# Decoder step: one PSUM bank per head in the weights-times-values, and grouped small products in both attentions

## The chip, the cores and the metric

The kernel runs on one core of a Trainium2 chip. The metric is device time in microseconds (us) of one execution; the time before is the median of three runs, 1080.63 us (1078.81 to 1083.95). Lower is better.

## The reference, cut to what matters

Two trunk layers of a decoder, for a prompt of 256 positions and 8 samples of 8 positions (320 columns in all, model width 1024), in fp32. Each layer is a mixer, then a cross-attention into 256 memory tokens with 4 heads of 256, then a squared-ReLU MLP. The mixer of layer 0 is gating plus retention; that of layer 1 is a sliding-window attention with 16 query heads and 4 key/value heads of 64.

```python
def cross_attend(h, mk, mv, w_mq, w_mo):
    q = (h @ w_mq).reshape(b, l, MEM_HEADS, MEM_HEAD_DIM)
    s = einsum('blhd,bmhd->bhlm', q, mk) * (MEM_HEAD_DIM ** -0.5)
    p = softmax(s)
    o = einsum('bhlm,bmhd->blhd', p, mv)
    return o.reshape(b, l, MEM_HEADS * MEM_HEAD_DIM) @ w_mo

def sink_attention(q, k, v, valid, sinks):
    s = einsum('...qkgd,...skd->...kgqs', q, k) * (C_HEAD_DIM ** -0.5)
    s = where(valid, s, -inf)
    p = softmax(concat([s, sink]))[..., :-1]
    return einsum('...kgqs,...skd->...qkgd', p, v)
```

The prompt attends to memory keys and values that the kernel computes itself (`mem_kv`); the samples attend to cached ones. In layer 1 the prompt attends to itself in blocks of 128, the samples to cached rows of 128 positions (`wk`, `wv`). A last RMSNorm gives `y`.

## The kernel before, in words

**Products.** X lies with features on partitions and the 320 columns in the free dimension. All large products are made in three passes with values split into a high and a low part: each weight block of 1 MB comes by one DMA from `ws` into one of three `stage` buffers (or, for the keys of the table `EXTRA`, into a free buffer of the tiles HH or HL), ACT rounds it to `whi`, DVE subtracts to `wlo` (two instructions of each per block, lines 143 to 147), and TensorE runs high by high, high by low and low by high. `gemm2` (line 188) takes such a block through 48 matmuls: 16 steps j of three. `gemm_tok` (line 214) does the same with the weights as the moving operand, 512 wide; a block is 24 matmuls there, in four steps of six, and j counts those as 0, 4, 8, 12.

**Order.** `hook(i, f, j=...)` (line 178) puts small work f behind step j of the i-th block from now; so the small products of the attentions stand between the matmuls of some large product that doesn't need them. The program order gives a priority; which instruction stands where in an engine's queue is fixed by the tile framework when the kernel is built, by its own estimate of when each is ready and when a buffer is free. Every engine runs its queue in order. Banks of PSUM come from two sets of four, `mm` for the large products and `at` for all others. `in_order` keeps the order as written. The plan (`_plan`, line 1390) lists the blocks in the order in which they are used; `weights` (line 157) stages and splits one block ahead, and stages up to two cached blocks that stand behind it.

**Cross-attention** (`cross`, line 586). For the samples, `kc` (line 469) multiplies cached keys with a block-diagonal tile Z: 16 matmuls for a block of 1 MB, four at a time in four 32-column strips of the array, all blocks of a pair of heads hp into one bank; `sample_softmax`, `sample_tr` (two transposes), then `vc` (line 541) the same way with cached values, whose fourth block scales the sum into the tile `ot`. For the prompt, `s1` makes scores and softmax, `s2` transposes the weights into PT (high part) and PL (low part), and `pv(hp)` (line 556) multiplies with the values: first two transposes of `ot` into a bank tp, then for each head of the pair and each half dc of its width a bank of its own, six matmuls 256 wide, an ACT copy to OH and a DVE subtraction to OL; last the copy and subtraction from tp into the columns 256 to 319 of OH and OL. `mo` (line 581) is the output product; its first matmul reads all 320 columns of OH of the first head, so it needs the copy from tp too. In layer 0 (`ahead` False) `kc(0,0)` and `kc(0,1)` are hooked into the last query product, `kc(0,2)` and `kc(0,3)` into the second key product, `vc(0,0)` and `vc(0,1)` into the last value block; the rest of the values work follows the value products. In layer 1 all of it stands behind the query products.

**Sliding attention** (lines 1111 to 1325). `w1(n, gp)` makes the scores of a block of 128 queries into four `at` banks and the softmax (DVE: add mask and take the maximum, later scale; ACT: exponentials) into one tile; `w2f(n, gp, kv)` turns one key/value head's weights by four transposes into a bank and copies it with ACT to a tile `pt` (tag `w2`, five buffers); `w3(n, gp, pr)` multiplies the turned weights of two heads with the values, two 64-column strips at a time, and copies to OH and OL. `ws_scores`, `ws_tr` and `ws_pv` do the same for the samples. Before, `w2f` comes in pairs and `w3` one by one, hooked into `qk_group` (N = 320), `mk` (N = 256) and `mv` (512 wide).

**End.** Three 128-row pieces of y (the last of 64 rows) are scaled in halves by DVE and ACT, and each half goes out by its own DMA of SP (lines 1385 and 1386).

Of the kernel before, what the change touches and what calls it, by code (L numbers as in the profile page):

```python
# [9 lines left out]
F32 = mybir.dt.float32  # L10
F32R = mybir.dt.float32r
I32 = mybir.dt.int32
AF = mybir.ActivationFunctionType
ALU = mybir.AluOpType
# [3 lines left out]
P = 128  # L18
NT = 320
NPR = 256  # L20
# [53 lines left out]
def decoder_step(ctx: ExitStack, tc: tile.TileContext, d, plan):  # L74
    nc = tc.nc
    V, A, G, T, S = nc.vector, nc.scalar, nc.gpsimd, nc.tensor, nc.sync
# [7 lines left out]
    def sb(shape, tag, bufs=1, dt=F32):  # L84
        cnt[0] += 1
        return pool.tile(list(shape), dt, tag=tag, bufs=bufs, name=f"{tag}_{cnt[0]}")

    def bank(kind="mm"):
        cnt[0] += 1
        return pmm.tile([P, 512], F32, tag=kind, bufs=4, name=f"{kind}_{cnt[0]}")  # L90
# [10 lines left out]
    def cvc(name, i=0, n=1):  # L101
# [6 lines left out]

    WEIGHTS = ("w_in", "w_out_e", "w_qkv", "w_out_o", "w_mq", "w_mk", "w_mv", "w_mo", "w_up", "w_down")
    EXTRA = {("vc", 0, 0, 0): "HH", ("vc", 0, 0, 1): "HL", ("vc", 0, 1, 0): "HH", ("vc", 0, 1, 1): "HL",  # L110
             ("vc", 1, 0, 0): "HH", ("vc", 1, 0, 1): "HL", ("vc", 1, 0, 2): "HH", ("vc", 1, 0, 3): "HL", ("mem",): "k8a"}
    at = [0]
    staged, halves = {}, {}
# [64 lines left out]
    def hook(i, *fs, j=7):  # L178
        while len(late) <= i:
            late.append([])  # L180
        late[i].extend((j, f) for f in fs)
# [259 lines left out]
    class Cross:  # L441
# [114 lines left out]
        def pv(self, hp):  # L556
            if hp == 0:
                self.OH = sb([P, KC, NT], "HH", 2, F32R)
                self.OL = sb([P, KC, NT], "HL", 2, F32R)
            tp = bank("at")  # L560
            for dc in range(2):
                T.transpose(tp[:, dc * P:(dc + 1) * P], self.ot[:, hp, dc * P:(dc + 1) * P], ident)
            for h2 in range(2):
                h = 2 * hp + h2
                for dc in range(2):
                    c = 2 * h + dc
                    po = bank("at")
                    for mc in range(2):
                        vh, vl = [t[:, mc, c * P:(c + 1) * P] for t in (self.VH, self.VL)]
                        T.matmul(po[:, :NPR], vh, self.PT[:, h, mc], start=(mc == 0), stop=False)  # L570
                        T.matmul(po[:, :NPR], vh, self.PL[h][:, mc], start=False, stop=False)
                        T.matmul(po[:, :NPR], vl, self.PT[:, h, mc], start=False, stop=(mc == 1))
                    A.activation(self.OH[:, c, :NPR], po[:, :NPR], AF.Copy)
                    V.tensor_tensor(self.OL[:, c, :NPR], po[:, :NPR], self.OH[:, c, :NPR].bitcast(F32), op=ALU.subtract)
            c = slice(4 * hp, 4 * hp + 4)
            oh, ol = [t[:, c, NPR:NT].rearrange("p (h d) t -> p h d t", h=2) for t in (self.OH, self.OL)]
            tv = tp[:, :256].rearrange("p (d h t) -> p h d t", d=2, h=2)
            A.activation(oh, tv, AF.Copy)
            V.tensor_tensor(ol, tv, oh.bitcast(F32), op=ALU.subtract)
# [6 lines left out]
    def cross(l, nm, mem, nn, ahead):  # L586
        c = Cross(l, nm, mem, nn)
        c.start()
        if not ahead:
            hook(2, lambda: in_order(mem.prep, (1,)))  # L590
            hook(3, lambda: in_order(mem.prep, (2,)))
        hook(3, lambda: c.kc(0, 0), lambda: c.kc(0, 1))
        if ahead:
            hook(0, lambda: ahead_of(("vc", 1, 0, 2), ("vc", 1, 0, 3)))
        for g in range(4):
            c.mq(g)
        if ahead:
            c.kc(0, 2)
            c.kc(0, 3)
            c.s1(0, 0)  # L600
            c.values(0)
            c.s1(1, 0)
            c.sample_softmax(0)
            c.kc(1, 0)
            c.kc(1, 1)
            c.values(1)
            c.s2(0, 0)
            c.s1(0, 1)
            c.sample_tr(0)
            c.s2(1, 0)  # L610
            c.s1(1, 1)
            c.kc(1, 2)
            c.kc(1, 3)
            c.s2(0, 1)
            c.vc(0, 0)
            c.vc(0, 1)
            c.sample_softmax(1)
            c.s2(1, 1)
            c.vc(0, 2)
            c.vc(0, 3)  # L620
            c.sample_tr(1)
        else:
            hook(1, lambda: c.kc(0, 2), lambda: c.kc(0, 3))
            hook(2, lambda: c.sample_softmax(0))
            hook(3, lambda: c.sample_tr(0), lambda: c.kc(1, 0), lambda: c.kc(1, 1))
            for g in range(4):
                mem.mk(g)
            hook(0, lambda: c.s1(0, 0))
            hook(1, lambda: c.kc(1, 2), lambda: c.kc(1, 3), lambda: c.s1(1, 0))
            hook(2, lambda: c.s2(0, 0), lambda: c.sample_softmax(1), lambda: c.s1(0, 1))  # L630
            hook(3, lambda: c.vc(0, 0), lambda: c.vc(0, 1), lambda: c.s2(1, 0), lambda: c.s1(1, 1),
                 lambda: c.sample_tr(1))
            mem.mv(0)
            hook(1, lambda: c.values(0), j=1)
            mem.mv(1)
            c.values(1)
            ahead_of(("vc", 0, 0, 2), ("vc", 0, 0, 3), ("vc", 0, 1, 0), ("vc", 0, 1, 1))
            c.vc(0, 2)
            c.vc(0, 3)
            c.s2(0, 1)  # L640
            c.s2(1, 1)
        ahead_of(("vc", l, 1, 0), ("vc", l, 1, 1), ("w_mo", l, 0, 0))
        c.vc(1, 0)
        c.vc(1, 1)
        c.pv(0)
        hook(1, lambda: c.vc(1, 2), lambda: c.vc(1, 3))
        c.mo(0, 0)
        c.mo(0, 1)
        c.pv(1)
        c.mo(1, 0)  # L650
        c.mo(1, 1)
        nn.finish()
# [56 lines left out]
    for c in (0, 1, 2, 4, 6):  # L709
        n = 1 if c < 2 else 2  # L710
# [469 lines left out]
    def w2f(n, gp, kv):  # L1180
        s = us.pop((n, gp, kv))
        tp = bank("at")
        pt = sb([P, 512], "w2", W2)
        for j in range(4):
            if n == 0:
                T.transpose(tp[:, j * P:(j + 1) * P], s[:, j], ident)
            else:
                T.transpose(tp[:, j * P:(j + 1) * P], s[:, j % 2, (j // 2) * P:(j // 2 + 1) * P], ident)
        A.activation(pt, tp, AF.Copy)
        up_[n, gp, kv] = pt  # L1190
# [111 lines left out]
        G.dma_start(d["wv_n"], VW[64:128, 2])  # L1302

    gemm_tok([("w_qkv", 5)], nm.h, nm.l, XS, 256, evac)
    hook(2, lambda: w1(1, 0, "k8b"), j=9)
    hook(3, lambda: w2f(1, 0, 0), lambda: w2f(1, 0, 1), j=9)
    hook(4, lambda: w3(1, 0, 0), lambda: w2f(1, 0, 2), lambda: w2f(1, 0, 3), rows_out, j=3)
    hook(4, lambda: w1(0, 0, "Z"), j=13)
    hook(5, lambda: w3(1, 0, 1), ws_prep, j=5)
    hook(6, lambda: w2f(0, 0, 0), lambda: w2f(0, 0, 1), j=3)  # L1310
    hook(6, lambda: w3(0, 0, 0), lambda: w2f(0, 0, 2), lambda: w2f(0, 0, 3), j=13)
    hook(7, lambda: w3(0, 0, 1), j=3)
    hook(7, lambda: w1(1, 1, "k8b"), j=9)
    for g in range(4):
        qk_group(g)
    for g in range(4):
        mem1.mk(g)
    hook(0, lambda: ws_scores(0), j=5)
    hook(1, lambda: w2f(1, 1, 0), lambda: w2f(1, 1, 1), j=1)
    hook(1, lambda: w3(1, 1, 0), lambda: w2f(1, 1, 2), lambda: w2f(1, 1, 3), lambda: ws_scores(1), j=9)  # L1320
    hook(2, lambda: w3(1, 1, 1), lambda: ws_tr(0))
    hook(3, lambda: ws_tr(1), j=3)
    hook(3, ws_pv, j=11)
    mem1.mv(0)
    mem1.mv(1)
# [54 lines left out]
    for j in range(3):  # L1380
        w = min(P, NT - j * P)
        r = slice(P - w, P)
        V.tensor_scalar(yo[r, j, :512], tp[0][j][r], rs[r, j:j + 1], None, op0=ALU.mult)
        A.activation(yo[r, j, 512:], tp[1][j][r], AF.Copy, scale=rs[r, j:j + 1])
        S.dma_start(d["y"][j * P:j * P + w, :512], yo[r, j, :512])
        S.dma_start(d["y"][j * P:j * P + w, 512:], yo[r, j, 512:])

def _plan():  # L1390
    p = []
# [9 lines left out]

    def mqk(l):
        return [("w_mq", l, 0), ("w_mq", l, 1)] + \
            [("w_mq", l, 2), ("w_mq", l, 3), ("kc", l, 0, 0), ("kc", l, 0, 1)]

    def mo(l):
        return [("vc", l, 1, 0), ("vc", l, 1, 1), ("w_mo", l, 0, 0), ("w_mo", l, 0, 1), ("vc", l, 1, 2), ("vc", l, 1, 3),
# [12 lines left out]

    p += mqk(0)
    for b in range(2):
        p += [("w_mk", 0, 2 * b), ("w_mk", 0, 2 * b + 1)] + [(("kc", 0, b, 2 - 2 * b + i)) for i in range(2)]
    p += [("w_mv", 0, 0, 0), ("w_mv", 0, 0, 1), ("kc", 0, 1, 2), ("kc", 0, 1, 3)]
    p += [("w_mv", 0, 1, 0), ("w_mv", 0, 1, 1)] + [("vc", 0, 0, b) for b in range(4)]
    p += mo(0) + mlp(0)
    p += [("w_qkv", 4), ("w_qkv", 5), ("w_qkv", 0), ("w_qkv", 1), ("w_qkv", 2), ("w_qkv", 3)]
    p += [("w_mk", 1, g) for g in range(4)] + [("w_mv", 1, 0, 0), ("wk",), ("w_mv", 1, 0, 1), ("w_mv", 1, 1, 0),
                                               ("w_mv", 1, 1, 1), ("wv",)]
    p += [("w_out_o", g) for g in range(4)] + mqk(1) + [("kc", 1, 0, 2), ("kc", 1, 0, 3)] + [("kc", 1, 1, b) for b in range(4)]  # L1430
    p += [("vc", 1, 0, b) for b in range(4)] + mo(1) + mlp(1)
# [197 lines left out]
```

## Time and profile before

| | before |
|---|---|
| median of three runs | 1080.63 us |
| the profiled execution: its time, its span | 1080.16 us, 1078.5 us |
| TensorE matmuls busy | 1066.8 us, 99% |
| weight loads busy | 1007.8 us, 93% |
| DVE busy, ACT busy, POOL busy | 702.5, 513.8, 63.7 us |
| chain that ended last: TensorE | 93% |
| moved by DMA | 201.39 MB, 187 GB/s on average |

The span is the time from the first to the last instruction of the program; the execution takes 1.66 us more. Matmuls overlap, so a matmul's own duration (0.31 us for 320 columns) is longer than the time from its start to the next one's start; what a matmul costs is read from starts. All instructions carry line 62 (the wrapper that calls them), so they are told apart by their tiles: `mm<-HH,whi` is a large product, `at<-stage,Z` a cached block, `at<-cst,XH` and its like the weights-times-values, `at<-ident,...` a transpose, `at<-w,cst` a `w3`.

### The profile page before, as it was taken

The numbers are of one execution on the slowest core, as the hardware profiler recorded it, in microseconds if no ns is written. First come the engines' busy times: TensorE is split into PE (matmuls) and PEld (weight loads), VectorE is DVE, ScalarE is ACT, GpSimd is POOL, SyncE is SP. The second block draws the span as 40 slices with busy tenths as digits, with TensorE's granted clock in tenths as the row PEclk, the third lists the DMA queues.
The fourth block names the chain that finished last, engine by engine and source line by source line (L and its number), as shares of the span: only waits on it lengthen the run. The fifth ranks groups of instructions, "written<-read, shape, count | busy, mean of one in ns | idle before, by whom it ended". The sixth has DMA issues, their size and how long they took to land.

```text
span 1078.5 us, 18402 instructions
## 1 busy us (share of the span) xinstructions
PE 1066.8 (99%) x7478; PEld 1007.8 (93%) x7478; DVE 702.5 (65%) x1376; ACT 513.8 (48%) x868; POOL 63.7 (6%) x74
## 2 busy tenths in 40 slices
PE   9999999999999999999999999999999999999997
PEld 9888989999977999999999999889969999999997
DVE  7878976876456676555556889757466865555543
ACT  7536632654344465343345456655144654443443
POOL 1000000020000110000001102002000200000001
PEclk9999999999999999999999999999999999999999
DMA  9533458645889644444444433847586444444421
GB/s 344 184 136 127 137 195 283 229 153 207 305 308 340 232 144 138 149 157 156 157 140 140 154 129 123 297 165 292 193 310 257 156 140 140 152 156 157 153 82 49
DMA packets 30486, 201.39 MB, mean 187 GB/s; under 512 B 3577, under 2 KB 4041, under 8 KB 7497
## 3 DMA queue, kind: packets, MB, share of 16 engines
q1 hardware_dynamic: 27600, 187.92, 49.6%
q0 software_dynamic: 2512, 11.54, 2.9%
q8 instruction: 59, 0.97, 0.4%
q10 hardware_dynamic: 288, 0.75, 0.2%
q14 instruction: 27, 0.21, 0.1%
HBM read 187.35 MB, written 12.85 MB: 186 GB/s over the span
## 4 chain that ended last, share of the span: by engine, by line
PE 93%; DMA 3%; DVE 2%; ACT 1%; issue 0%; SPq 0%; DVEq 0%; ACTq 0%
PE mm L62 81%; PE at L62 11%; DMA stage<-ws 3%; DVE wlo L62 1%; ACT whi L62 1%; ACT k8b L62 0%; DVE cst L62 0%; ACT w L62 0%; DVE sm_mx L62 0%; DVE XL L62 0%; ACT XH L62 0%; SPq L705 0%; DVE k L62 0%; DVE HL L62 0%; DVEq L1602 0%
## 5 line engine op out<-in xcount | busy, mean ns | idle before, releaser
L62 ACT ACTIVATE whi<-stage 128x1024 fp32r<-128x1024 f32 (+1 forms) x269 | 280.4, 1054 | 382.5 <-PE mm L62 281.5
L62 DVE TENSOR_TENSOR wlo<-stage,whi 128x1024 fp32r<-128x1024 f32 (+1 forms) x269 | 326.4, 1222 | 185.3 <-ACT whi L62 179.7
L62 PE MATMUL mm<-HL,whi 128*128 128x320 f32 (+1 forms) x960 | 292.8, 305 | 0.6 <-DVE HL L62 0.6
L62 PE MATMUL mm<-HH,whi 128*128 128x320 f32 (+1 forms) x960 | 293.1, 307 | 0.0
L62 PE MATMUL mm<-HH,wlo 128*128 128x320 f32 (+1 forms) x960 | 292.6, 305 | 0.0
L62 PE MATMUL mm<-XH,whi 128*128 128x320 f32 x896 | 279.2, 312 | 0.0
L62 PE MATMUL mm<-XL,whi 128*128 128x320 f32 x896 | 276.9, 309 | 0.0
L62 PE MATMUL mm<-XH,wlo 128*128 128x320 f32 x896 | 276.5, 309 | 0.0
L62 PEld LDWEIGHTS mm<-HH,whi 128*128 128x128 f32 x960 | 180.1, 188 | 4.0 <-issue 2.8
L62 PEld LDWEIGHTS mm<-HL,whi 128*128 128x128 f32 x960 | 180.5, 188 | 1.1 <-DVE HL L62 0.9
L62 PEld LDWEIGHTS mm<-HH,wlo 128*128 128x128 f32 x960 | 180.5, 188 | 0.0
L62 PEld LDWEIGHTS mm<-XH,whi 128*128 128x128 f32 x896 | 168.3, 188 | 2.4 <-issue 2.0
L62 PEld LDWEIGHTS mm<-XL,whi 128*128 128x128 f32 x896 | 168.3, 188 | 0.5
L62 PEld LDWEIGHTS mm<-XH,wlo 128*128 128x128 f32 x896 | 168.1, 188 | 0.1
L62 DVE TENSOR_TENSOR X<-mm,X 128x320 f32<-128x320 f32 x112 | 51.8, 489 | 53.3 <-PE mm L62 53.1
L62 POOL TENSOR_TENSOR ssq<-ssq,sqt 128x320 f32<-128x320 f32 x36 | 38.1, 1058 | 625.4 <-ACT sqt L62 624.5
L62 ACT ACTIVATE t<-t 128x320 f32<-128x320 f32 x80 | 34.3, 461 | 23.1 <-DVE t L62 23.0
L62 DVE SCALAR_TENSOR_TENSOR t<-mm,RB 128x320 f32<-128x320 f32 x64 | 30.2, 490 | 22.0 <-PE mm L62 21.6
L62 DVE TENSOR_TENSOR HL<-t,HH 128x320 fp32r<-128x320 f32 x80 | 36.8, 486 | 10.5 <-ACT HH L62 9.9
L62 DVE SCALAR_TENSOR_TENSOR XL<-X,cv,XH 128x320 fp32r<-128x320 f32 x48 | 37.9, 810 | 5.7 <-ACT XH L62 5.7
L62 ACT ACTIVATE HH<-t 128x320 fp32r<-128x320 f32 x80 | 34.7, 462 | 11.2 <-DVE t L62 10.6
L62 ACT ACTIVATE XH<-X,cv 128x320 fp32r<-128x320 f32 x48 | 26.4, 554 | 22.1 <-DVE X L62 19.5
(267 smaller groups left out, 1055.1 us busy)
## 6 DMA issues: line engine op xcount, KB each, us to landing
stage<-ws SPq DMA_DIRECT2D x161, 1024.0 KB, 4.9
o_ret_s<-stage POOLq DMA_DIRECT2D x8, 512.0 KB, 6.5
HH<-ws SPq DMA_DIRECT2D x4, 1024.0 KB, 7.1
HL<-ws SPq DMA_DIRECT2D x4, 1024.0 KB, 6.9
k8a<-ws SPq DMA_DIRECT2D x2, 1024.0 KB, 8.2
o_mem_k<-k8a POOLq DMA_DIRECT2D x2, 1024.0 KB, 8.7
o_mem_v<-k8b POOLq DMA_DIRECT2D x2, 1024.0 KB, 11.8
stage<-ws SPq DMA_DIRECT2D x3, 512.0 KB, 7.9
```

The source lines that it names most:

```text
L62: r = f(*a, **k)
```

## The change

In `pv`, the two halves of a head share one bank (12 matmuls, then one copy and one subtraction, 512 wide), and the two transposes of `ot` come behind both heads. In layer 0 all four `kc(0,b)` are hooked into the last query product, two of their blocks go to HH and HL, `sample_softmax(0)` moves up one hook, and all four `vc(0,b)` come behind the value products. In the sliding attention the four `w2f` of a block come together (`turned`), the two `w3` together (`summed`), `ws_scores` and `ws_tr` in pairs, and the places of the hooks change. Each piece of y goes out by one DMA. The plan follows.

```diff
     EXTRA = {("vc", 0, 0, 0): "HH", ("vc", 0, 0, 1): "HL", ("vc", 0, 1, 0): "HH", ("vc", 0, 1, 1): "HL",
+             ("kc", 0, 0, 2): "HH", ("kc", 0, 0, 3): "HL",
...
+            for h in range(2 * hp, 2 * hp + 2):
+                po = bank("at")
+                for dc in range(2):
+                    c = 2 * h + dc
+                    for mc in range(2):
+                        vh, vl = [t[:, mc, c * P:(c + 1) * P] for t in (self.VH, self.VL)]
+                        o = po[:, dc * NPR:(dc + 1) * NPR]
+                        T.matmul(o, vh, self.PT[:, h, mc], start=(mc == 0), stop=False)
+                        T.matmul(o, vh, self.PL[h][:, mc], start=False, stop=False)
+                        T.matmul(o, vl, self.PT[:, h, mc], start=False, stop=(mc == 1))
+                ov = po.rearrange("p (c t) -> p c t", c=2)
+                oh, ol = [t[:, 2 * h:2 * h + 2, :NPR] for t in (self.OH, self.OL)]
+                A.activation(oh, ov, AF.Copy)
+                V.tensor_tensor(ol, ov, oh.bitcast(F32), op=ALU.subtract)
             tp = bank("at")
             for dc in range(2):
                 T.transpose(tp[:, dc * P:(dc + 1) * P], self.ot[:, hp, dc * P:(dc + 1) * P], ident)
-            for h2 in range(2):
...
-                    po = bank("at")
...
-                    A.activation(self.OH[:, c, :NPR], po[:, :NPR], AF.Copy)
-                    V.tensor_tensor(self.OL[:, c, :NPR], po[:, :NPR], self.OH[:, c, :NPR].bitcast(F32), op=ALU.subtract)
...
-        hook(3, lambda: c.kc(0, 0), lambda: c.kc(0, 1))
+        hook(3, *[lambda b=b: c.kc(0, b) for b in range(2 if ahead else 4)])
...
-            hook(1, lambda: c.kc(0, 2), lambda: c.kc(0, 3))
-            hook(2, lambda: c.sample_softmax(0))
+            hook(1, lambda: c.sample_softmax(0))
...
-            hook(3, lambda: c.vc(0, 0), lambda: c.vc(0, 1), lambda: c.s2(1, 0), lambda: c.s1(1, 1),
-                 lambda: c.sample_tr(1))
+            hook(3, lambda: c.s2(1, 0), lambda: c.s1(1, 1), lambda: c.sample_tr(1))
...
-            c.vc(0, 2)
-            c.vc(0, 3)
+            for b in range(4):
+                c.vc(0, b)
...
+    def turned(n, gp):
+        for kv in range(4):
+            w2f(n, gp, kv)
+
+    def summed(n, gp):
+        for pr in range(2):
+            w3(n, gp, pr)
+
     hook(2, lambda: w1(1, 0, "k8b"), j=9)
-    hook(3, lambda: w2f(1, 0, 0), lambda: w2f(1, 0, 1), j=9)
-    hook(4, lambda: w3(1, 0, 0), lambda: w2f(1, 0, 2), lambda: w2f(1, 0, 3), rows_out, j=3)
+    hook(3, lambda: turned(1, 0), j=11)
+    hook(4, lambda: summed(1, 0), rows_out, j=5)
     hook(4, lambda: w1(0, 0, "Z"), j=13)
-    hook(5, lambda: w3(1, 0, 1), ws_prep, j=5)
-    hook(6, lambda: w2f(0, 0, 0), lambda: w2f(0, 0, 1), j=3)
-    hook(6, lambda: w3(0, 0, 0), lambda: w2f(0, 0, 2), lambda: w2f(0, 0, 3), j=13)
-    hook(7, lambda: w3(0, 0, 1), j=3)
-    hook(7, lambda: w1(1, 1, "k8b"), j=9)
+    hook(5, ws_prep, j=5)
+    hook(5, lambda: turned(0, 0), j=15)
+    hook(6, lambda: summed(0, 0), j=9)
+    hook(7, lambda: w1(1, 1, "k8b"), j=3)
...
-    hook(0, lambda: ws_scores(0), j=5)
-    hook(1, lambda: w2f(1, 1, 0), lambda: w2f(1, 1, 1), j=1)
-    hook(1, lambda: w3(1, 1, 0), lambda: w2f(1, 1, 2), lambda: w2f(1, 1, 3), lambda: ws_scores(1), j=9)
-    hook(2, lambda: w3(1, 1, 1), lambda: ws_tr(0))
-    hook(3, lambda: ws_tr(1), j=3)
+    hook(0, lambda: turned(1, 1), j=3)
+    hook(0, lambda: summed(1, 1), j=13)
+    hook(1, lambda: ws_scores(0), lambda: ws_scores(1), j=9)
+    hook(2, lambda: ws_tr(0), lambda: ws_tr(1), j=11)
     hook(3, ws_pv, j=11)
...
-        S.dma_start(d["y"][j * P:j * P + w, :512], yo[r, j, :512])
-        S.dma_start(d["y"][j * P:j * P + w, 512:], yo[r, j, 512:])
+        S.dma_start(d["y"][j * P:j * P + w], yo[r, j])
...
-            [("w_mq", l, 2), ("w_mq", l, 3), ("kc", l, 0, 0), ("kc", l, 0, 1)]
+            [("w_mq", l, 2), ("w_mq", l, 3)] + [("kc", l, 0, b) for b in range(2 if l else 4)]
...
-        p += [("w_mk", 0, 2 * b), ("w_mk", 0, 2 * b + 1)] + [(("kc", 0, b, 2 - 2 * b + i)) for i in range(2)]
+        p += [("w_mk", 0, 2 * b), ("w_mk", 0, 2 * b + 1)] + [("kc", 0, 1, i) for i in range(2) if b]
...
-    p += [("w_mk", 1, g) for g in range(4)] + [("w_mv", 1, 0, 0), ("wk",), ("w_mv", 1, 0, 1), ("w_mv", 1, 1, 0),
+    p += [("w_mk", 1, g) for g in range(4)] + [("w_mv", 1, 0, 0), ("w_mv", 1, 0, 1), ("wk",), ("w_mv", 1, 1, 0),
```

## Rows read from the trace of the kernel before

**Rows 1.** The page, part 4: shares of the chain that ended last, by engine.

```profile
PE 93%; DMA 3%; DVE 2%; ACT 1%; issue 0%; SPq 0%; DVEq 0%; ACTq 0%
```

**Rows 2.** Table by stage: from:to, length, busy by engine, clock, DMA, GB/s.

```profile
331.00:345.00 14.00, 13.19 (x125) 9.92 (x124) 11.10 (x30) 8.17 (x17) 0.54 (x1) 1.00 0.98 374
```

**Rows 3.** Timeline (start, us, instruction), TensorE, layer 0: `vc` inside `mo`.

```profile
353.00 0.31 PE L62 MATMUL mm<-HL,whi 128*128 128x320 f32 x1
353.14 0.31 PE L62 MATMUL mm<-HH,wlo 128*128 128x320 f32 x1
353.38 1.93 PE L62 MATMUL at<-stage,Z 128*32 128x256 f32 x32
355.25 0.42 PE L62 MATMUL mm<-HH,whi 128*128 128x320 f32 x1
355.50 0.31 PE L62 MATMUL mm<-HL,whi 128*128 128x320 f32 x1
```

**Rows 4.** Timeline, TensorE, layer 0: `vc(0,0)`, `vc(0,1)`, then `s2`.

```profile
326.27 1.07 PE L62 MATMUL at<-HH,Z 128*32 128x256 f32 x16
327.16 1.05 PE L62 MATMUL at<-HL,Z 128*32 128x256 f32 x16
328.14 0.66 PE L62 MATMUL at<-ident,w 128*128 128x128 f32 x4
```

**Rows 5.** Timeline, TensorE, layer 1: two `w2f`; one `w3` with `w2f` behind.

```profile
646.67 1.03 PE L62 MATMUL at<-ident,k8b 128*128 128x128 f32 x8
647.46 0.40 PE L62 MATMUL mm<-XH,whi 128*128 128x320 f32 x1
647.69 0.31 PE L62 MATMUL mm<-XL,whi 128*128 128x320 f32 x1
...
651.70 1.08 PE L62 MATMUL at<-w,cst 128*64 128x256 f32 x8
652.71 1.09 PE L62 MATMUL at<-ident,k8b 128*128 128x128 f32 x8
```

**Rows 6.** Timelines: TensorE's first matmul behind `w1(0,0)`; DVE's last scaling of it.

```profile
659.25 0.39 PE L62 MATMUL mm<-HH,whi 128*128 128x256 f32 x1
...
669.38 0.86 DVE L62 TENSOR_SCALAR Z<-Z,w_sm 128x128 f32<-128x128 f32 x4
```

**Rows 7.** Timeline, TensorE, layer 0: waits before `pv(0)` and inside `pv(1)`.

```profile
338.75 0.44 PE L62 MATMUL at<-ident,k 128*128 128x128 f32 x2 [0.46 <-DVE k L62]
339.50 0.47 PE L62 MATMUL at<-cst,XH 128*128 128x256 f32 x2 [0.32 <-DVE XL L62]
...
362.22 0.39 PE L62 MATMUL at<-cst,XH 128*128 128x256 f32 x1 [0.81 <-DVE HL L62]
```

**Rows 8.** Timeline, TensorE, layer 1: wait behind `pv(0)`; both ends of `pv(1)`.

```profile
811.34 0.41 PE L62 MATMUL mm<-HL,whi 128*128 128x320 f32 x1 [0.62 <-DVE HL L62]
...
824.36 0.38 PE L62 MATMUL at<-ident,k 128*128 128x128 f32 x2
...
827.33 0.28 PE L62 MATMUL at<-cst,XL 128*128 128x256 f32 x1
827.45 0.46 PE L62 MATMUL mm<-HH,whi 128*128 128x320 f32 x2
```

**Rows 9.** Timeline, ACT, layer 1: split during `pv(0)`; copy from tp in `pv(1)`.

```profile
808.63 1.06 ACT L62 ACTIVATE whi<-stage 128x1024 fp32r<-128x1024 f32 x1 [1.48 <-DMA stage<-ws]
...
824.78 0.39 ACT L62 ACTIVATE HH<-at 128x256 fp32r<-128x256 f32 x1 [5.22 <-PE at L62]
```

**Rows 10.** Groups, 605 to 830 us: 512-wide subtraction, copy (busy us, mean ns).

```profile
L62 DVE TENSOR_TENSOR HL<-at,HH 128x512 fp32r<-128x512 f32 x2 | 1.4, 692 | 1.7 <-ACT HH L62 1.7
...
L62 ACT ACTIVATE HH<-at 128x512 fp32r<-128x512 f32 x2 | 1.2, 598 | 3.5 <-PE at L62 3.5
```

**Rows 11.** The page, part 6 (KB, us to landing): HH; SP's last y issue.

```profile
HH<-ws SPq DMA_DIRECT2D x4, 1024.0 KB, 7.1
...
1074.44 0.57 SPq L1386 DMA_DIRECT2D o_y<-cst  x1
```

More of the change, by code (lines that the diff above doesn't have):

```diff
@@ L562, in pv @@
                 T.transpose(tp[:, dc * P:(dc + 1) * P], self.ot[:, hp, dc * P:(dc + 1) * P], ident)
-            for h2 in range(2):
-                h = 2 * hp + h2
-                for dc in range(2):
-                    c = 2 * h + dc
-                    po = bank("at")
[L568 to L572, printed above, removed]
-                    A.activation(self.OH[:, c, :NPR], po[:, :NPR], AF.Copy)
-                    V.tensor_tensor(self.OL[:, c, :NPR], po[:, :NPR], self.OH[:, c, :NPR].bitcast(F32), op=ALU.subtract)
             c = slice(4 * hp, 4 * hp + 4)
```

## The prediction

> **What bounds the kernel now.** I read the chain of waits first: 93% of the span is TensorE [rows 1]. So work of ACT, DVE or a DMA costs only where TensorE then waits, and the change is worth what it takes from or adds to TensorE's queue. The table by stage comes second: even in the tightest stretch, behind the value products of layer 0, TensorE is busy 13.19 of 14.00 us at full clock, though DMA stands at 0.98 there [rows 2]. Third come the timelines at each place touched. No matmul is dropped; what can go is the cost of switching between kinds of matmul, and waits.
>
> *A switch.* A 320-wide matmul starts 0.14 us after the one before. Into a block of `vc` it takes 0.24, and the first matmul behind takes 0.25 [rows 3]: 0.10 each. Of two blocks of `vc` in a row, the second takes 0.98 us where the first takes 0.89 [rows 4]: 0.09 more where the strips end. A visit to the strips thus costs 0.29 us beside its work. A visit of transposes costs nothing: eight take 0.79, and the matmul behind them 0.09 more than normal [rows 5], 0.11 each in all, which they take in a row too.
>
> **The change, part by part.** The sum is against the profiled execution, 1080.16 us (span 1078.5 and 1.66 around it), 0.47 below the median shown.
>
> *Grouped `w3`, cached rows by fours.* Three pairs of `w3` become one visit each. One visit of two goes: 0.29 if it returned to large products, 0.19 where transposes stood behind it [rows 5] and the last 0.10 is not paid; I take 0.25, 0.75 for three. `kc(0,2)` and `kc(0,3)` join the first two: 0.29. `vc(0,0)` and `vc(0,1)` leave the last value block for a place where strips run anyway: 0.25. Grouping `w2f`, `ws_scores` and `ws_tr`: nothing. **Together -1.29** (-1.1 to -1.5). What moves with them: two key loads go to HH and HL, which stand free early, and the two value loads that stood there come later instead; SP issues as many as before, and the three stage buffers are less pressed. `sample_softmax(0)` moves one hook up (one maximum, one exponential, covered by a 5 us product). The send of the cached rows, issued by POOL inside `ws_scores(0)`, moves back by one value block; behind it on POOL stand other sends and the clearing of Z, not read until the next query product, over 40 us on. No one waits.
>
> *Turned weights.* `turned(0,0)` stands 18 steps of three 256-wide matmuls behind `w1(0,0)`: at 0.12 each (827.33 to 827.45 in [rows 8]), 6.5 us after 659.25 [rows 6], at 665.7. Its last four of sixteen transposes come 1.3 later, at 667.0; the softmax was scaled only at 670.24 [rows 6], 3.2 us too late. `turned(1,1)` has less room than before too and gets the same bound; `turned(1,0)` has 18 steps of 320 and fits. The upper end is 6.4. The lower is 0: the framework may leave large matmuls in front until it thinks the softmax ready. Nothing is idle before the transposes of [rows 5], so its estimate was good there; I take **+0.5**, near that row. Behind waiting transposes the whole of TensorE's queue stands.
>
> *Weights times values, what goes.* Layer 0 waits 0.46 before `pv(0)` for `ot` and 0.32 for a bank that `s2` still held [rows 7]. An idle stretch understates by 0.16, since a 256-wide matmul lasts 0.28 and the next may start after 0.12 [rows 8]: 0.94 in all. Two more blocks of `vc` now stand in front and `ot` is read later, so both go. Inside `pv(1)` the fourth bank was waited for 0.81, so 0.97; three banks now do, of four. In layer 1, 0.62 (0.78) was waited behind `pv(0)` [rows 8] because a copy stood on ACT behind a split that waited 1.48 for its load [rows 9]. That load comes no earlier, so I take half, 0.4. **Together -2.31** (-1.9 to -2.7).
>
> *Weights times values, what comes.* The transposes of `ot` are now last, and `mo` needs their copy in its first matmul. Before, this copy ran beside the heads: in layer 1 the transposes started at 824.36, the copy at 824.78 [rows 8, 9], and `mo` followed `pv(1)` with no gap [rows 8]. Now, with T the start of the second head's last matmul: the 512-wide copy of that head starts at T + 0.42 and takes 0.60 [rows 10], the copy from tp 0.39 more [rows 9]: T + 1.41. Without waiting `mo` would start at T + 0.42 (two transposes). So **1.0 us, four times: +4.0**. The low part, a 0.69 subtraction and one from tp, is covered: two high matmuls went ahead of the low one in [rows 8]. Lower end: ACT takes tp first, T + 0.93, 0.5 each, 2.0. Upper end: a split of 1.06 [rows 9] stands before each copy, 8.2. I take 1.0, since in three of four places no load is waited for. What stands behind the waiting matmul is all of `mo`, then the norm and the MLP; no hooked work lies within the first block of `mo`.
>
> No row shows a copy out of a bank into which matmuls still go. The Trainium skill (PSUM — Partial Sum Buffer, section PSUM bank collisions) has TensorE and a reader kept apart by whole bank and quadrant, so the first half of a shared bank cannot be copied while the second is written. By this rule the copy is one of 0.60; were it not so, a 0.39 copy would be left at the end, 0.8 us would be waited each time, and the sum would be 0.8 us lower.
>
> *Loads behind the move.* `vc(1,0)` loads into HH. Before, that buffer was free once `vc(0,0)` had read it, at 327.2 [rows 4]. Now `vc(0,0)` comes behind the value products, and from its end to `vc(1,0)` there are three blocks (0.94) and eight transposes, 3.7 us, against 7.1 to land [rows 11]: 3.4 late at most. At least 0: the first head of `pv(0)` may go ahead, and another buffer of HH is free as the value products end. I take **+0.5**, near the lower end.
>
> *Three transfers of y.* SP's issues were 0.57 each at the end [rows 11]; the last piece now needs one less: **-0.6** (-1.2, were all three spared at the end, to 0 if the memory is the limit).
>
> Sum: -1.29 + 0.5 - 2.31 + 4.0 + 0.5 - 0.6 = +0.8. **Forecast 1081.0 us**, 0.4 above the median shown: no change.
>
> **The rivals.**
> - *Stacked transposes wait for the softmax* (slower). Place: the head of TensorE's queue at `turned(0,0)` and `turned(1,1)`; price 6.4 instead of 0.5: 1086.9. It decides once the order fixed at build puts sixteen transposes at their hook while DVE scales as late as before. For it: the 3.2 above, and that ACT's queue was fixed against a load that came late [rows 9]. Against: no idle in [rows 5].
> - *The new wait is half hidden* (faster). ACT copies tp first or near so, 2.0 instead of 4.0, the wait of [rows 8] goes whole (0.4) and y gives 0.6 more: 1078.0. For it: ACT has half as many copies from `pv` as before.
> - *The late load.* 3.4 instead of 0.5: 1083.9. For it: DMA at 0.98 [rows 2].
> - *The groups are not kept.* The framework fixes the order by its estimates and tears `summed` apart; the 0.75 falls away: 1081.7.
>
> **How the numbers follow.** About 0.5%, 5.4 us, is what a measurement of this kernel can tell from no change. Chances: forecast 0.37, stacked transposes 0.15, half hidden 0.26, late load 0.12, groups torn 0.10. The last two and the forecast stay within 5.4 us but for their edges. Slower by more, above 1086.0: a little over half of the first rival and 0.03 of others, 0.12. Faster by more, below 1075.2: of the half hidden wait 0.08, if the waits of layer 0 were worth more than their rows, and 0.03 of others, 0.11. The range, 1076.5 to 1086.0, holds the forecast with its bounds one at a time (-2.0 and +4.2), the half hidden wait less its tail, and under half of the stacked transposes.
>
> **What would show it.** Right: two strip visits fewer for each count above; in all four `pv`, an idle stretch of about 0.8 us of TensorE before the first `mm<-HH,whi`, released by ACT; none inside `pv(1)` of layer 0. Wrong: no such idle (then faster), or idle before `at<-ident,Z` or `at<-ident,k8b` released by DVE, or before `at<-HH,Z` released by a DMA (then slower).

## The result and the profile after

The changed kernel takes 1089.07 us (median of five, 1087.94 to 1090.65); the kernel before took 1079.21 in the same measuring. The ratio, which is taken over all runs and is not that of the two medians, is 1.0083 [1.0072, 1.0094]: slower, by 9.9 us between the medians, and 3 us above the range forecast. The profiled execution is the longest of the five, 1090.65 us with a span of 1088.9.

Where it went is read from the start of the all-ones matmul of each norm in the timeline of TensorE; the stretch between two of them is a stage.

| stage | before | after | difference |
|---|---|---|---|
| up to the norm of the cross-attention, layer 0 | 246.35 | 247.94 | +1.59 |
| cross 0: from there to the norm of the MLP | 136.93 | 140.91 | +3.98 |
| MLP of layer 0 | 224.95 | 224.95 | 0 |
| mix 1: layer 1 with the sliding attention | 147.38 | 148.45 | +1.07 |
| cross 1 | 92.20 | 96.29 | +4.09 |
| MLP of layer 1 | 219.67 | 219.69 | +0.02 |
| end, with y | 10.96 | 10.64 | -0.32 |

The first line is not the change's: TensorE's order is the same there, and over the twelve kernels profiled this stage took 245.66 to 247.94 us. What is left is 8.8 us, in the two `pv` and the sliding attention. Part 4 of the page after, the chain that ended last (before: [rows 1]):

```profile
PE 91%; DMA 4%; DVE 3%; ACT 1%; issue 1%; SPq 0%; DVEq 0%; POOL 0%; ACTq 0%; POOLq 0%
```

TensorE gave up two points to loads and to DVE. Where, the timelines show.

**Tail of layer 0.** Timeline of TensorE after (before: [rows 4, 7]):

```profile
335.98 1.09 PE L62 MATMUL at<-ident,w 128*128 128x128 f32 x8
339.66 1.07 PE L62 MATMUL at<-HH,Z 128*32 128x256 f32 x16 [2.58 <-DMA HH<-ws]
...
344.72 1.07 PE L62 MATMUL at<-HL,Z 128*32 128x256 f32 x16 [1.52 <-DMA HL<-ws]
...
347.54 0.86 PE L62 MATMUL mm<-HH,whi 128*128 128x320 f32 x4
348.33 0.62 PE L62 MATMUL at<-stage,Z 128*32 128x256 f32 x2
```

`vc(1,0)` is waited for, then `vc(1,1)`, and two matmuls of `vc(1,2)` are a visit of their own. The waits for `ot` and for a bank [rows 7] are gone; from 326 us to the end of this `mo` TensorE loses 4.8 us against the kernel before. SP's timeline shows when the load of HH was sent (that of HL follows it), first after, then before:

```profile
332.26 0.33 SPq L131 DMA_DIRECT2D HH<-ws  x1
```

```profile
327.40 0.33 SPq L130 DMA_DIRECT2D HH<-ws  x1
```

What this did to the DMA engines is in the table by stage (columns as in [rows 2]), first after, then before:

```profile
326.00:332.00 6.00, 6.00 (x31) 5.00 (x30) 3.57 (x7) 3.44 (x7) 0.00 (x0) 1.00 0.22 90
336.00:340.00 4.00, 1.42 (x20) 1.15 (x20) 3.41 (x4) 3.37 (x5) 0.14 (x1) 1.00 1.01 360
```

```profile
326.00:332.00 6.00, 6.00 (x55) 4.28 (x54) 3.08 (x6) 3.51 (x7) 0.00 (x0) 1.00 0.86 322
```

Before the stretch in which DMA stands at 1.0, the memory now idles: 0.22 where it was 0.86, 3.8 us of transfers not made (6 x 0.64), because HH and HL come free only at 332. The two loads are sent there, behind a stage load sent at 331.6, with the write of `mem_v` (sent at 335.6) beside them, and land 7.3 and 12.0 us later; before, they landed 5.0 and 6.6 us after they were sent.

**The copy out of tp.** Three of the four `pv` show the forecast wait: behind `pv(1)` in layer 0, behind both in layer 1. Timeline of TensorE behind `pv(1)` of layer 0 and `pv(0)` of layer 1:

```profile
367.81 0.86 PE L62 MATMUL mm<-HH,whi 128*128 128x320 f32 x4 [0.74 <-ACT HH L62]
369.08 0.42 PE L62 MATMUL mm<-HL,whi 128*128 128x320 f32 x1 [0.41 <-DVE HL L62]
...
814.84 0.85 PE L62 MATMUL mm<-HH,whi 128*128 128x320 f32 x4 [0.74 <-ACT HH L62]
```

The timelines behind `pv(1)` of layer 1 (before: [rows 8, 9]), of TensorE, then ACT, then DVE:

```profile
833.96 0.38 PE L62 MATMUL at<-ident,k 128*128 128x128 f32 x2
835.69 0.85 PE L62 MATMUL mm<-HH,whi 128*128 128x320 f32 x4 [1.35 <-ACT HH L62]
837.42 0.64 PE L62 MATMUL mm<-HL,whi 128*128 128x320 f32 x1 [0.89 <-DVE HL L62]
837.86 0.47 PE L62 MATMUL mm<-HH,wlo 128*128 128x320 f32 x1
838.12 0.47 PE L62 MATMUL mm<-HL,whi 128*128 128x320 f32 x1
```

```profile
832.38 1.06 ACT L62 ACTIVATE whi<-stage 128x1024 fp32r<-128x1024 f32 x1 [6.25 <-DMA stage<-ws]
833.35 0.58 ACT L62 ACTIVATE HH<-at 128x512 fp32r<-128x512 f32 x1
833.83 1.05 ACT L62 ACTIVATE whi<-stage 128x1024 fp32r<-128x1024 f32 x1
834.77 0.86 ACT L62 ACTIVATE HH<-at 128x512 fp32r<-128x512 f32 x2
```

```profile
833.48 1.23 DVE L62 TENSOR_TENSOR wlo<-stage,whi 128x1024 fp32r<-128x1024 f32 x1 [0.97 <-ACT whi L62]
834.62 0.68 DVE L62 TENSOR_TENSOR HL<-at,HH 128x512 fp32r<-128x512 f32 x1
835.22 1.22 DVE L62 TENSOR_TENSOR wlo<-stage,whi 128x1024 fp32r<-128x1024 f32 x1
836.35 1.02 DVE L62 TENSOR_TENSOR HL<-at,HH 128x512 fp32r<-128x512 f32 x2
```

The copies stand behind two splits on ACT, the first of which had waited for its load, and the subtractions behind two on DVE. So `mo` waits twice, and then its matmuls start 0.27 us apart instead of 0.15. The table by stage says why; the clock is the column behind POOL:

```profile
836.00:838.00 2.00, 1.11 (x6) 0.85 (x5) 1.37 (x3) 0.00 (x0) 0.00 (x0) 0.75 0.76 188
838.00:840.00 2.00, 2.00 (x10) 2.00 (x9) 0.00 (x0) 0.00 (x0) 0.00 (x0) 0.50 0.85 348
840.00:842.00 2.00, 2.00 (x14) 2.00 (x14) 0.14 (x1) 0.00 (x0) 0.00 (x0) 0.89 0.28 115
```

The granted clock fell to 0.50, the 1.2 GHz level, at 837.0 and rose again at 840.4. From the start of this `pv` to the norm 3.25 us are lost; `pv(0)` loses 0.85, net of the wait of [rows 8], which went whole.

**Sliding attention.** Timelines of TensorE at `turned(1,1)`, then of DVE (before, its two halves: eight transposes each without a wait, as in [rows 5]):

```profile
691.43 1.47 PE L62 MATMUL at<-ident,k8b 128*128 128x128 f32 x12
694.03 0.33 PE L62 MATMUL at<-ident,k8b 128*128 128x128 f32 x1 [1.12 <-DVE k8b L62]
694.11 0.48 PE L62 MATMUL mm<-whi,HH 128*128 128x512 f32 x1
694.43 0.49 PE L62 MATMUL at<-ident,k8b 128*128 128x128 f32 x3
```

```profile
692.48 1.22 DVE L62 TENSOR_TENSOR wlo<-stage,whi 128x1024 fp32r<-128x1024 f32 x1
693.63 0.61 DVE L62 TENSOR_SCALAR k8b<-k8b,w_sm 128x256 f32<-128x256 f32 x2
```

Twelve transposes go ahead, the thirteenth waits for the scaled softmax, which stands behind a split on DVE. `turned(0,0)` is torn: its sixteen transposes lie in nine pieces among large products from 672.3 to 676.8. `turned(1,0)` does not wait.

### The profile page after: what moved, and what is told of

Same layout as the page of the kernel before. It is cut to its first block, busy times and chain, and to the rows that moved or that the text cites. A ratio compares the mean times of both kernels' runs of the same rounds, so it can differ in the third digit from the quotient of the medians.

```text
span 1088.9 us, 18396 instructions
## 1 busy us (share of the span) xinstructions
PE 1068.9 (98%) x7478; PEld 1009.2 (93%) x7478; DVE 702.7 (65%) x1368; ACT 512.8 (47%) x860; POOL 64.3 (6%) x74
## 4 chain that ended last, share of the span: by engine, by line
PE 91%; DMA 4%; DVE 3%; ACT 1%; issue 1%; SPq 0%; DVEq 0%; POOL 0%; ACTq 0%; POOLq 0%
PE mm L62 80%; PE at L62 12%; DMA stage<-ws 2%; DMA HL<-ws 1%; DVE wlo L62 1%; DMA X<-x 0%; DMA o_ret_s<-stage 0%; DVE k8b L62 0%; ACT whi L62 0%; DVE HL L62 0%; DVE stage L62 0%; DVE cst L62 0%; ACT L62 0%; DVE nw_u L62 0%; ACT k8b L62 0%
```

## The experiments

Each expectation sets theories, named by a letter, against each other. Theory W: all three moves cost, through waits. The table has the stages in which the profiles differ. Ratios are to runs of the kernel before made beside each run (their medians: 1080.07 us for e1 to e4, 1079.59 for e5 to e8, 1079.53 for e9 and e10). The last two columns tell for how many us the granted clock stood at 0.50 in cross 0 and in cross 1; from the first to the last of the norms it was 1.00 everywhere else.

| kernel | median us | ratio [95%] | cross 0 | mix 1 | cross 1 | 0.50 in cross 0 | 0.50 in cross 1 |
|---|---|---|---|---|---|---|---|
| before | 1079.21 | 1 | 136.93 | 147.38 | 92.20 | 0 | 0 |
| after | 1089.07 | 1.0083 [1.0072, 1.0094] | 140.91 | 148.45 | 96.29 | 0 | 3.4 |
| e1_ot_first | 1084.29 | 1.0032 [1.0020, 1.0044] | 140.82 | 148.41 | 92.39 | 3.4 | 0 |
| e2_rows_early | 1088.46 | 1.0061 [1.0037, 1.0084] | 140.37 | 148.44 | 96.43 | 3.4 | 3.4 |
| e3_slide_before | 1088.22 | 1.0063 [1.0045, 1.0082] | 141.11 | 147.41 | 94.92 | 3.4 | 0 |
| e4_three_back | 1080.04 | 0.9995 [0.9981, 1.0010] | 136.32 | 147.41 | 92.38 | 0 | 0 |
| e5_between | 1080.69 | 1.0006 [0.9997, 1.0016] | 139.39 | 147.41 | 91.70 | 3.4 | 0 |
| e6_rows_early_held | 1087.14 | 1.0067 [1.0052, 1.0081] | 140.65 | 148.47 | 95.07 | 6.8 | 0 |
| e7_groups_due | 1081.83 | 1.0019 [1.0007, 1.0032] | 141.53 | 147.03 | 91.70 | 6.8 | 0 |
| e8_before_ot_last | 1083.92 | 1.0040 [1.0028, 1.0052] | 137.73 | 147.35 | 95.90 | 0 | 3.4 |
| e9_mixed | 1078.36 | 0.9987 [0.9978, 0.9997] | 136.76 | 147.13 | 91.69 | 0 | 0 |
| e10_before_rows_late | 1082.10 | 1.0020 [1.0009, 1.0032] | 138.95 | 147.38 | 92.22 | 3.4 | 0 |

**One thing undone: `ot` first.**

```diff
+            tp = bank("at")      # and its two transposes
             for h in range(2 * hp, 2 * hp + 2):
...
-            tp = bank("at")      # and its two transposes
```

> The changed kernel with one thing undone: in all four pv the transposes of ot stand in front of the heads again (the shared banks stay). Theory W (waits): the two traces give a loss of 0.85 us by the end of pv(0) in layer 1 and of 3.25 us from pv(1) of layer 1 to the root of its norm, where TensorE waits 1.62 and 1.19 us for the copies out of tp and then runs matmuls at 0.27 us that took 0.14; about nothing in pv(1) of layer 0. So 1089.1 - 4.1 = 1085.0 us, no wait of over 0.3 us between the transposes and the first 320-wide matmul, and no matmul at half speed in pv(1) of layer 1. The tail of layer 0 keeps its waits for loads. Rival L (loads): the first wait in pv(1) of layer 1 ends with a split that was itself 6.25 us late for its load, so that only the waits for the copies go and the load keeps TensorE waiting: 1.5 us less at most, 1087.5 us. Rival S (sliding attention): the loss lies in the torn groups; nothing changes, 1089 us.

1084.29 us, as W said, and of the stages it is cross 1 that gains: -3.90, with no fall of the clock; of the waits one of 0.72 us for a subtraction is left. L falls: the late split by itself keeps nobody waiting for long. Cross 0 gains 0.09. Its timeline at `vc(1,0)`:

```profile
339.47 1.72 PE L62 MATMUL at<-HH,Z 128*32 128x256 f32 x16 [3.55 <-DMA HH<-ws]
```

HH was sent 85.1 us after the norm here (at 331.85), 84.3 in the changed kernel, and landed 7.5 us later, for 7.3, so the wait for it grew by 1.0. The wait for HL (1.52) is gone, but the clock stood at 0.50 from 339.8 to 343.2. Behind `pv(1)` the waits for ACT and DVE are 0.46 and 0.77, for 0.74 and 0.41. Both kernels begin `mo` 99.6 us after the norm: here the loads set the pace, and the place of `ot` does not.

**One thing undone: `vc(0,0)`, `vc(0,1)` early.**

```diff
-            hook(3, lambda: c.s2(1, 0), lambda: c.s1(1, 1), lambda: c.sample_tr(1))
+            hook(3, lambda: c.vc(0, 0), lambda: c.vc(0, 1), lambda: c.s2(1, 0), lambda: c.s1(1, 1),
+                 lambda: c.sample_tr(1))
...
-            for b in range(4):
-                c.vc(0, b)
+            c.vc(0, 2)
+            c.vc(0, 3)
```

> The changed kernel with one thing undone: vc(0,0) and vc(0,1) of layer 0 stand in the last block of value products again. Theory W: in the tail of layer 0 TensorE waits 2.9 and 1.8 us for the two loads of vc(1,0) and vc(1,1), which are sent when vc(0,0) and vc(0,1) have read HH and HL; sent five us earlier, they land in time and both waits go; the wait for the copies out of tp in pv(0), now hidden behind the second load wait, shows with up to 1.0 us. The tail lost 4.8 us in all; 1089.1 - 3.8 = 1085.3 us (1084.3 if the wait for the copies stays hidden). Rival M (the memory): the loads are at the limit of the DMA engines and land no earlier; at most 1 us less, 1088 us.

W was wrong by 3 us: cross 0 won 0.54. M had the time, but not for its reason: HH and HL landed early and in time (332.5 and 335.0). But behind `pv(0)` the timeline of TensorE has

```profile
341.49 0.38 PE L62 MATMUL at<-ident,k 128*128 128x128 f32 x2
344.51 0.63 PE L62 MATMUL at<-stage,Z 128*32 128x256 f32 x6 [2.64 <-DMA stage<-ws]
```

The order fixed at build put matmuls of `vc(1,2)` into the gap that the copy out of tp leaves, and their load landed 2 us after the copy. One late thing took the other's place. Behind it the clock stood at 0.50 from 345.2 to 348.6, where the changed kernel had 1.00; by its price in cross 1 (next run) this is 1.4 of the 3 us, an estimate.

**One thing undone: the sliding attention.** The hooks and the place of `wk` in the plan are those of before.

> The changed kernel with one thing undone: hooks and order of loads of the sliding attention as before the change. Theory W: from the first w1 to ws_pv the changed kernel lost 1.0 us against the one before; 1089.1 - 1.0 = 1088.1 us, and the stretch between them as long as before. Rival S: what the late groups push back (outputs of ACT and DVE, loads) also makes the waits of layer 1, so that 3 us and more go: 1086 us or less.

1088.22 us, mix 1 as before (147.41). Cross 1 was 1.37 shorter too, though its waits behind `pv(1)` are the same, in the timeline and in the table by stage:

```profile
833.42 0.85 PE L62 MATMUL mm<-HH,whi 128*128 128x320 f32 x4 [1.31 <-ACT HH L62]
835.16 0.41 PE L62 MATMUL mm<-HL,whi 128*128 128x320 f32 x1 [0.89 <-DVE HL L62]
```

```profile
835.73:837.73 2.00, 2.00 (x15) 2.00 (x15) 0.00 (x0) 0.00 (x0) 0.00 (x0) 1.00 0.76 319
```

TensorE's order in cross 1 is that of the changed kernel. The clock did not fall here; that is the price of the fall, 1.4 us. In cross 0, where the order is the same too, it is the other way about. Timeline of TensorE and table by stage of this run, then the table of the changed kernel:

```profile
338.15 1.07 PE L62 MATMUL at<-HH,Z 128*32 128x256 f32 x16 [2.52 <-DMA HH<-ws]
```

```profile
339.30:342.70 3.40, 3.40 (x17) 3.40 (x18) 0.92 (x4) 0.60 (x1) 0.00 (x0) 0.50 1.01 417
```

```profile
340.00:344.00 4.00, 3.19 (x35) 2.52 (x26) 2.59 (x6) 0.60 (x1) 0.00 (x0) 1.00 0.98 393
```

Cross 0 is only 0.20 longer with the fall: the slower matmuls filled the time for which the changed kernel waited for HL (1.52).

**All three undone.** The three diffs together.

> The changed kernel with the three things undone together (ot first, vc(0,0) and vc(0,1) early, sliding attention as before); what is left of the change are the shared banks of pv, the keys by fours and the three transfers of y. Theory W: 1089.1 - 4.1 - 4.8 - 1.0 = 1079.2 us, and since waits for ot and for banks of the kernel before do not come back with the shared banks (about 1 us) and keys and y give 0.3 each, 1077.5 to 1079.2 us: as the kernel before or a little faster. If it stays above 1081 us, shared banks, keys or y cost time by themselves, against what the traces show.

1080.04 us, a ratio of 0.9995: the three moves are the loss. In cross 0 they don't add up. Rows early wins 4.50 where `ot` is first (140.82 to 136.32) and 0.54 where it is last; `ot` first wins 4.05 with rows early and 0.09 with rows late. The clock has a part in this: it fell in cross 0 of each run with one thing undone, and in this one nowhere.

**`ot` between the heads.** To the run with all three undone:

```diff
             V.tensor_tensor(ol, ov, oh.bitcast(F32), op=ALU.subtract)
+            if h == 2 * hp:
+                tp = bank("at")      # and its two transposes
```

> As the run with three things undone, but the transposes of ot stand between the two heads of each pv: the matmuls of the first head may run while ot is scaled on DVE, and those of the second while the copies out of tp run. Theory W: the 0.79 and 0.59 us that TensorE waited on both sides of the transposes in front of pv(0) of layer 0 go, and nothing is waited for behind the second head but its own copy: 1080.0 - 1.3 = 1078.7 us. Rival C (copies): in layer 0 the last copy of 0.60 us is then alone in front of mo as well as behind the heads; what is won in front is waited for behind, 1080 us.

Against that run cross 1 became 0.68 shorter, cross 0 3.07 longer: the waits before `pv(0)` went, and TensorE waited 2.19 us for `vc(1,2)` instead and 1.16 for a subtraction behind `pv(1)`; from 343.6 to 347.0 the clock stood at 0.50. In layer 0 the loads set the pace, in layer 1 not.

**`vc(1,2)`, `vc(1,3)` held at their place.** To the run with rows early:

```diff
-        hook(1, lambda: c.vc(1, 2), lambda: c.vc(1, 3))
+        hook(1, lambda: in_order(c.vc, 1, 2), lambda: in_order(c.vc, 1, 3))
```

> The changed kernel with vc(0,0) and vc(0,1) early, as before, and besides with vc(1,2) and vc(1,3) of both layers held at their place in the program, so that no matmul of theirs stands between the transposes of ot and mo. Theory G (gap filler): without the hold TensorE stood 2.64 us idle before the first matmul of vc(1,2), whose load landed at 344.46 us, while the copies out of tp had ended by 342.6; held, only the wait for the copies is left, 1.0 us: 1088.5 - 1.9 = 1086.6 us. Rival C: the copies themselves are late and the load only ends with them; then nothing changes, 1088.5 us.

The time, 1087.14 us, lies between G and C. Behind `pv(0)` G came true (1.02 us from the second transpose to the next matmul instead of 2.9), but cross 0 did not shorten (140.65). TensorE reached the end of `pv(1)` 4 us earlier, while the splits there still stood in front of the copies; its timeline, and the table by stage:

```profile
361.62 0.85 PE L62 MATMUL mm<-HH,whi 128*128 128x320 f32 x4 [0.85 <-ACT HH L62]
364.15 0.64 PE L62 MATMUL mm<-HL,whi 128*128 128x320 f32 x1 [1.68 <-DVE HL L62]
364.59 0.47 PE L62 MATMUL mm<-HH,wlo 128*128 128x320 f32 x1
```

```profile
364.00:366.00 2.00, 1.85 (x7) 1.85 (x8) 0.10 (x1) 0.00 (x0) 0.00 (x0) 0.50 0.98 282
366.00:368.00 2.00, 2.00 (x9) 2.00 (x8) 0.00 (x0) 0.00 (x0) 0.00 (x0) 0.50 0.79 324
368.00:370.00 2.00, 2.00 (x9) 2.00 (x9) 0.37 (x1) 0.00 (x0) 0.00 (x0) 0.50 0.02 8
```

Here the clock stayed at 0.50 for some 22 matmuls, 0.12 us each: 2.6 us.

**Groups at their due times.** To the run with `ot` between the heads:

```diff
+    hook(6, lambda: turned(0, 0), j=9)
+    hook(7, lambda: summed(0, 0), j=3)
...
+    hook(1, lambda: turned(1, 1), lambda: ws_scores(1), j=5)
+    hook(2, lambda: summed(1, 1), lambda: ws_tr(0), j=3)
```

> The kernel with the transposes of ot between the heads, and besides the groups of the sliding attention, each at the place where the later half of its work stood before the change: turned(1,0) 11 steps into the third block, turned(0,0) in the middle of the seventh, turned(1,1) in the second block of value products, summed a hook behind each. Theory W: groups cost only where they stand ahead of the softmax; here sixteen transposes run in a row, and the three visits of w3 less give the 0.75 us of the prediction: 0.7 us less than the same kernel with the old order of the sliding attention, about 1078 us. Rival S: sixteen transposes fill all four banks, so that they or the products wait for copies wherever they stand: no gain, or up to 1 us of loss.

Mix 1 is 0.38 shorter than with the old order: the groups win half of what W said. The median is higher all the same, because of cross 0, which this edit leaves as it was: `vc(1,2)` landed at 344.9 instead of 343.0, its wait was 3.42 us instead of 2.19, and the clock stayed at 0.50 until 350.4 instead of 347.0. Table by stage of this run, then of the one with `ot` between the heads:

```profile
347.00:350.40 3.40, 3.40 (x14) 3.40 (x15) 0.00 (x0) 0.00 (x0) 0.00 (x0) 0.50 0.77 253
```

```profile
347.10:350.40 3.30, 3.30 (x25) 3.30 (x24) 0.94 (x2) 0.00 (x0) 0.00 (x0) 1.00 0.91 338
```

So executions differ by 2 us where loads set the pace: the four runs of this kernel whose mean granted clock was 0.998 or more took 1078.28 to 1080.30 us, the other eight 1081.04 to 1085.23. The profile is one of the eight.

**`ot` last, alone.** To the kernel before: the transposes stand behind the heads, nothing else.

> The kernel before with one thing changed alone: in all four pv the transposes of ot stand behind the heads (banks, rows, sliding attention, keys and y as before). Theory P (price of the prediction): a wait of 1.0 us for the copies out of tp in each of the four pv and nothing else: 1080.1 + 4.0 = 1084.1 us, less up to 1 us that was waited for ot before. Theory W: the wait also lets work in front of mo that itself waits (vc(1,2) for its load in layer 0), comes behind splits on ACT and DVE in layer 1, and brings TensorE to half speed there: 4 us in each layer, 1088 us. Rival B (banks): it is the shared bank that keeps the copies back, since the copy of a whole head starts only with its last matmul; with four banks of half the size the wait is 0.6 us each and less, 1082.5 us or below.

P gave the time (1083.92) but not the places: +0.80 in cross 0, where waits for `ot` went and one of 1.49 for `vc(1,2)` came, +3.70 in cross 1. The timeline of ACT in `pv(0)` of layer 1:

```profile
809.37 1.06 ACT L62 ACTIVATE whi<-stage 128x1024 fp32r<-128x1024 f32 x1 [1.65 <-DMA stage<-ws]
810.33 0.64 ACT L62 ACTIVATE HH<-at 128x256 fp32r<-128x256 f32 x2
```

A split that waits for its load stands before the last copies; `mo` waits 1.82 us for them, and the clock stands at 0.50 from 811.1 to 814.5. B falls as the main cause, as the loss comes without a shared bank. What a bank shared adds shows where no split stands in the way: from the transposes to `mo` 0.80 us in `pv(1)` of layer 0 here, 1.02 with the shared bank.

**Rows late, alone.** To the kernel before: the reverse of the second diff.

> The kernel before with one thing changed alone: vc(0,0) and vc(0,1) of layer 0 stand behind the value products, and so the loads of vc(1,0) and vc(1,1) into HH and HL come later. Theory W: with ot first the four kinds of runs so far differ by 4.5 us in this stage between rows early and rows late; here too TensorE waits some 3.8 us for HH and 0.5 us and more for HL, less 0.25 for the visit saved and up to 0.9 that was waited for ot: 1079.6 + 3.5 to 4.2, 1083 to 1084 us. Rival P (price of the prediction): 0.5 us, 1080.1 us; 3.4 us at most, because HH is sent when the first block is read and three blocks and eight transposes stand between.

1082.10 us, cross 0 +2.02: four times P, under W. TensorE waits for HH as in the changed kernel, by its timeline:

```profile
338.00 1.07 PE L62 MATMUL at<-HH,Z 128*32 128x256 f32 x16 [2.44 <-DMA HH<-ws]
```

Behind this wait the clock stood at 0.50 from 339.9 to 343.3, and TensorE came to HL after it had landed (342.4). The move costs about as much without a fall: three of the eleven runs had a mean granted clock of 0.999 and took 1081.44 to 1082.13 us.

**The best form of each part.** Rows early; `ot` first in layer 0, between the heads in layer 1; groups at their due times; keys, banks and y of the changed kernel.

> Of each part of the change the form that cost least in the runs so far: keys by fours, shared banks and three transfers of y as in the changed kernel; vc(0,0) and vc(0,1) early and ot first in layer 0 (stage of 136.3 us against 136.9 of the kernel before); ot between the heads in layer 1 (91.7 against 92.2); the sliding attention in groups at their due times (147.0 against 147.4); the end 0.3 shorter. Theory W: the stages add up, 1.8 us less than the kernel before, 1077.9 us. Rival R (chance of the loads): the loads of each execution land otherwise, and the stages differ by as much between executions of one program; 1079 to 1080 us, not told from the kernel before.

1078.36 us, ratio 0.9987 [0.9978, 0.9997]: 1.2 us less than the kernel before, of the 1.8 that the stages promised. It is the fastest kernel here, by less than the 0.5% of the prediction's bound.

## Why the prediction was wrong

It had 1081.0 with a range to 1086.0. By stage it had +0.05 in cross 0, -0.25 in mix 1, +1.6 in cross 1 and -0.6 at the end; measured were +3.98, +1.07, +4.09 and -0.32.

- **Loads behind the move, +0.5: the step that failed most.** In place of 0.5, TensorE stood idle 4.1 us for these loads in the changed kernel. The bound itself was near for HH: 3.4 at most, against 2.58 idle after, 2.44 in the run with this alone and 3.55 with `ot` first. In part this is luck: the load was sent as the value products ended, 1.0 us before `vc(0,0)` had read its block, and the 7.1 is the median of four loads, of which this one took 5.0 before and 7.3 after. It left out HL, which lands behind HH in a full memory (1.52 more), and I took the lower end because a buffer of HH "is free as the value products end". It is, at 332, but a load sent there still comes late. Alone the move costs 2.0 us with its saved visit; beside `ot` first 4.5, between a profile with a fall of the clock and one without.
- **Weights times values, what comes, +4.0: place and wait right, price too low.** The chain comes out a little short of T + 1.41 where ACT is free: `mo` starts at T + 1.24, 1.02 us behind the second transpose, in `pv(1)` of layer 0 and `pv(0)` of layer 1. That the low part "is covered" failed: it was waited for 0.41 in `pv(1)` of layer 0, and 0.89 in `pv(1)` of layer 1, where both subtractions stood behind splits. The upper end had a split before each copy; it came true in that one `pv`, which I had counted among the three where "no load is waited for". And no term had the clock: 1.4 us. In cross 1 the wait costs 3.9 in this profile, 2.5 without the fall, instead of 2.0.
- **What goes, -2.31: right.** The changed kernel has none of the waits of [rows 7, 8], and the one of layer 1 went whole. But in layer 0 this only brings TensorE earlier to a load, as the runs with `ot` between the heads and with `ot` last alone show (2.19 and 1.49 us for `vc(1,2)`).
- **Turned weights, +0.5: the mechanism of the first rival, at the other place.** `turned(0,0)`, worked out as 3.2 late, was torn by the order fixed at build and not waited for; `turned(1,1)` waited 1.12. Against a gain of 0.38 measured for groups in time, the places chosen cost about 1.4.
- **Grouped work, -1.29.** The keys gave 0.34 for 0.29 (TensorE's delay against before falls from 1.59 to 1.25 us across the merged visit). The groups gave 0.38 for 0.75. The rival *The groups are not kept* did not come for `summed`: each pair of `w3` is one visit.
- **Three transfers of y, -0.6:** 0.32 in each profile that has them.
- **The shared bank.** From the second transpose to `mo` it takes 1.02 us with the shared bank and 0.80 with half banks, the 0.2 a place that the prediction gave for it. The Trainium skill (PSUM — Partial Sum Buffer, section PSUM bank collisions) has software guard PSUM by bank and quadrant. No run tests this rule: the changed kernel copies a head by one instruction, which needs both halves in any case, and the prediction's 0.60 follows from that alone.

The rival *late load* was the right one for layer 0, with chance 0.12 and a price that left out the second load; no rival had the copies behind splits in layer 1 or the clock. Of the signs asked for, these came: the idle before the first `mm<-HH,whi` released by ACT in three of the four `pv`, none inside `pv(1)` of layer 0, and both kinds of wrong idle, before `at<-k8b` by DVE and before `at<-HH,Z` by a DMA.

Open: the parts alone give 0.80 + 2.02 - 0.34 = 2.5 us in cross 0, together 4.0. That the rest is the memory's, where every arrival depends on the one before, is argued and not shown; the 2.02 holds a stretch at 0.50, the 4.0 none. Keys and y were not run alone.

## What to carry to other kernels

Where DMA stands near 1.0 ahead, ask of each moved read not only whether its own data come in time, but when the buffer that it frees is filled again, and let the memory not idle before the tight stretch. Put an operation whose result must be copied for the next product ahead of work that does not need it; last in line, it makes TensorE wait for all that stands in the copying engines' queues. Where a stage is paced by loads, a wait taken away comes back at the next load, so the worth of two such edits is not their sum. Before a difference between two single profiles is put down to an edit, compare the granted clock of the two in that stage.

## What was not expected of the hardware

The granted clock fell in cross 0 or cross 1 in nine of the twelve profiles; the three without a fall are those of the three fastest kernels. Each fall began in a wait of TensorE or less than 2 us behind one, but the waits alone do not settle whether it comes. The changed kernel and the run with the old sliding attention have the same order of TensorE in both stages. In cross 0 the clock fell behind a wait of 2.52 us for HH in the second, and not behind one of 2.58 in the first. In cross 1 it fell in the first, with waits of 1.35 and 0.89, and not in the second, with 1.31 and 0.89. At that place it fell in the run with rows early too (1.30 and 0.88), and not in the one with `vc(1,2)` held (1.47 and 0.89).

The Trainium skill (TensorE: Matmul & The Clock Gate, section HAM oscillation — how this bites in real kernels) tells of a kernel whose TensorE is throttled by each of its waits for loads. Here waits for copies (1.35 and 0.89) were followed by a fall as well, and a wait for a load (2.58) was not.

For the price of a wait this means a spread: on top of it come 0.2 us in cross 0, where a load would have been waited for otherwise, 1.4 in cross 1 and an estimated 2.6 in the run with `vc(1,2)` held, where the clock stayed at 0.50 for 6.8 us. The falls are not the main part of the loss: the one run of the changed kernel with a mean granted clock of 0.999 took 1087.94 us, the other four (0.996 to 0.997) 1088.94 to 1090.65.
